# Triangular inversion by 16-blocks, one per partition, laid out by strided 32x32 transposes on VectorE, with one more join, and scans 4 steps apart

## The chip, the cores and the metric

The kernel runs on one core of a Trainium2 chip. The metric is the time of one execution on the device, in microseconds. Before the change it is 3477.72 us, the median of three runs that reach from 3461.62 to 3479.61 us.

## The reference

Everything is fp32, with 256 tokens and a model width of 2048. Two hybrid attention layers come first, then one trunk layer with two recurrent branches (an rwkv7 and a gated delta net), each run in both directions over a context and over the latent tokens, then a merge, a squared-relu MLP and a norm:

```python
for l in range(2):                      # first block
    x = x + concat(fox, diff, moba, gla attention of rms_norm(x) @ w_in[l]) @ w_out[l]
x = rms_norm(x, final_norm_g)
p, pc = modulate(rms_norm(x)) @ in_w, modulate(rms_norm(ctx)) @ in_w   # second block
ya = rwkv7_branch(p, pc); yb = gdn_branch(p, pc)
x = x + g1 * ((gate_a * (ya @ up_a) + gate_b * (yb @ up_b)) @ out_w)
x = x + g2 * (square(relu(modulate(rms_norm(x)) @ mlp_w1)) @ mlp_w2)

# rwkv7_scan, 16 heads of 64, over the tokens, for each direction
sa = S @ kk_t
S = S * dec_t - outer(sa, b_t) + outer(v_t, k_t);   y_t = S @ r_t

# gdn_chunked, 8 heads of 128, chunks of 64 tokens
a_mat = tril(kb @ k.T * decay, -1) + eye(64)
u, w = triangular_solve(a_mat, [v * beta, kb * exp(gc)], lower=True, unit_diagonal=True)
```

The kernel computes both recurrences in chunks of 128 tokens. Written so, each chunk needs the inverse of a unit triangular 128x128 matrix (the identity plus a strictly triangular part), for every head, chunk and direction.

## The kernel before

**Projections.** Most of the work is projections of the tokens by streamed weights. A 128x512 piece of weights is loaded into `wr`, ScalarE casts it to the upper part `wh` (L230) and VectorE subtracts to get the lower part `wl` (L231). For each 128x128 part PE then runs three matmuls into `pp`: upper weights by upper activations (L171), upper by lower (L172), lower by upper (L173). The few `wh` and `wl` buffers are used in turn, so PE stops a little after ScalarE or VectorE stops casting. The row of PE then names `act`, the activations, and `wh` or `wl`.

**Scans.** `scans` (L1637) runs the recurrences as Python generators, four `rwkv` calls (four heads each) and two `gdn` calls (four heads each) for the context ("c"), then the same for the latent tokens ("x"): 12 calls in all. Two calls are alive at a time, in slot 0 and slot 1, and step by turns. The second starts `LEAD` turns after the first (L1641, L1644). The scans are issued at a higher priority than the projections (L1891), which fill what the scans leave.

**What sets the order.** A planner takes the instructions by their priority and by a model of their durations, and writes out one queue per engine (PE, VectorE = DVE, ScalarE = ACT, GpSimd = POOL, SyncE = SP). On the chip every engine then works through its own queue in that fixed order: an instruction that must wait holds up all that stands behind it on its engine. Buffers come from rings: a tile of a tag with `bufs` buffers can be written only when the tile that held the same buffer has been used for the last time. `NN` = 3 is the ring of the tag `nat`, which both slots use, `NL` = 3 that of `LX`.

**One inversion.** Each call inverts 16 matrices of 128x128 at once: 8 (`u`) for each of two directions (`d`), in the tile `nt`, in place. `nt` is filled from score products, which are L1274 in `rwkv` and L1543 in `gdn`. Then `invert` (L1066) does the following.

- VectorE negates the four diagonal 32x32 blocks of each matrix (L1076, L1077), and a 32x32 transpose (L1078) turns those of one direction, so that all have one orientation in `pk`.
- A DMA writes `pk` to DRAM (L1083, `iva`), and two read it back as `X` (L1088), in such a way that one partition holds one 32x32 block: 64 blocks, and each stands on two partitions, one for the even columns and one for the odd. ScalarE copies each partition's 16 columns into `own` (L1093).
- GpSimd does a forward substitution in 30 steps of a multiply (L1099) and an add (L1100). The generator yields every five steps.
- A DMA writes the result to DRAM (L1105, `ivb`), and two read it back as `ivo` in the layout of `nt` (L1113). ScalarE merges even and odd columns into `xb` (L1114), and VectorE transposes it (L1115): now the inverted diagonal blocks are in SBUF both ways.
- First join, 32 to 64: PE multiplies blocks of `nt` by inverted ones (L1126), ScalarE copies from PSUM (L1128), PE multiplies again (L1133, L1134), and ScalarE and VectorE put the parts in place (L1139 to L1145).
- Second join, 64 to 128: the same with 64x64 blocks (L1152, L1154, L1158, L1161).

The small products of the joins use `tile_position`, so that four 32x32 products lie in one matmul array at different places. They are fp32 products, not of the rounded type of the projections.

**The end of the scans.** The last `gdn` call reads its output out through transposes on PE (L1632) and writes `yb` to DRAM. `merge` (L1689) loads it again as `ytb` (L1694), splits it into `yb` pieces, and starts the projection by `up_b`.

Of the kernel before, what the change touches and what calls it, by code (L numbers as in the profile page):

```python
# [9 lines left out]
F32 = mybir.dt.float32  # L10
# [3 lines left out]
AF = mybir.ActivationFunctionType  # L14
ALU = mybir.AluOpType
AX = mybir.AxisListType
# [12 lines left out]

N1, N2, NM = 6, 5, 4  # L30

LEAD = 8

PP, S0, S1 = 3, 3, 2

SCANS = 4000

NN, NL = 3, 3

R0, R1, R2 = 3, 2, 3  # L40

XO = (800, 300, 240, 200)
# [800 lines left out]
class Second:  # L843
# [192 lines left out]
    def scan_consts(self):  # L1036
# [11 lines left out]
        for d in range(2):  # L1048
            sg = 1 if d == 0 else -1
            for base, lst, n in ((-1, self.mst, "mst"), (0, self.min, "min")):  # L1050
                sel(f, on, [[sg, 128]], base, -sg)
                u = c(f"{n}{d}", [128, 128], U8)
                v.tensor_copy(u, f)
                lst.append(u)
        self.srd = [e.t([128, 2, 2, 128], f"srd{j}", 1) for j in range(2)]
        for x in self.srd:
            g.memset(x, 0.0)
# [6 lines left out]
    def invert(self, nt, par):  # L1064
# [9 lines left out]
        iv = lambda n, shape: e.t(shape, n, NN, tag="nat")  # L1074
        for b in range(4):
            v.tensor_scalar(tmp[q(b)], nt[q(b), 0, :, q(b)], -1.0, None, op0=MUL)  # L1076
            v.tensor_scalar(pk[q(b), 1], nt[q(b), 1, :, q(b)], -1.0, None, op0=MUL)  # L1077
        v.transpose(pk[:, 0].rearrange("p u c -> p (u c)"), tmp.rearrange("p u c -> p (u c)"))  # L1078
        da = e.dp.tile([64, 1024], F32, name="iva", tag="iva", bufs=2)
        db = e.dp.tile([128, 512], F32, name="ivb", tag="ivb", bufs=2)  # L1080
        ap = lambda d, *l: bass.AP(tensor=d[:, :].tensor, offset=d[:, :].offset, ap=[list(x) for x in l])

        nc.sync.dma_start(ap(da, (32, 128), (4096, 16), (1, 32)), pk.rearrange("p d u c -> p (d u) c"))  # L1083


        X = e.t([128, 1024], "X", NL, tag="LX")
        for b in range(2):
            nc.sync.dma_start(X[hf(b)], da)  # L1088
        Xm = X.rearrange("p (i j) -> p i j", j=32)
        O = e.t([128, 512], f"own{par}", 1)  # L1090
        Om = O.rearrange("p (i m) -> p i m", m=16)
        for b in range(2):
            s.copy(Om[hf(b)], X.rearrange("p (i m b) -> p i m b", m=16, b=2)[hf(b), :, :, b])  # L1093
        g.memset(O[hf(1), 16:512:33], 0.0)
        yield
        for j in range(1, 31):
            n, w = 31 - j, (j + 1) // 2
            t = e.t([128, 256], f"sub{par}", 1)[:, :n * w].rearrange("p (i c) -> p i c", c=w)
            g.tensor_tensor(t, bc(Xm[:, j + 1:, j], w, 2), bc(Om[:, j, :w], n, 1), op=MUL)  # L1099
            g.tensor_tensor(Om[:, j + 1:, :w], Om[:, j + 1:, :w], t, op=ADD)  # L1100
            if j % 5 == 4:
                yield
        for b in range(2):
            g.memset(O[hf(b), 16 * b:512:33], 1.0)
        nc.sync.dma_start(db, O)  # L1105
        big = e.t([128, 1024], "xb", NL, tag="LX")
        xd, xt = (big[:, i:i + 512].rearrange("p (d u c) -> p d u c", d=2, u=8) for i in (0, 512))

        d64 = e.t([128, 8, 64], "d64", NN, tag="nat")
        g.memset(d64, 0.0)  # L1110
        own = iv("ivo", [128, 16, 2, 16])
        for b in range(2):
            nc.sync.dma_start(own[:, :, b], bass.AP(tensor=db[:, :].tensor, offset=db[:, :].offset + 32768 * b, ap=[[16, 128], [2048, 16], [1, 16]]))  # L1113
        s.copy(big[:, :512].rearrange("p (e m b) -> p e b m", e=16, b=2), own)  # L1114
        v.transpose(xt.rearrange("p d u c -> p (d u c)"), xd.rearrange("p d u c -> p (d u c)"))  # L1115
        db_ = [xd[:, 0], xt[:, 1]]
        xb = [xt[:, 0], xd[:, 1]]
        yield
# [802 lines left out]
```

## Time and profile before

| | |
|---|---|
| median of three runs | 3477.72 us (3461.62 to 3479.61) |
| the profiled execution | 3466.57 us, span 3464.9 us |
| PE (TensorE matmuls) busy | 3271.6 us, 94% of the span |
| PEld (weight loads, beside PE) busy | 2998.4 us, 87% |
| VectorE busy | 2357.9 us, 68% |
| ScalarE busy | 1576.6 us, 46% |
| GpSimd busy | 548.3 us, 16% |
| mean granted TensorE clock | 0.968 of full speed |

The span is the time from the first to the last instruction of one profiled execution. An engine's busy time is the time in which it executes something, its waits and its queue's own work excluded. These shares are means over all stages; the scans lie between about 1200 and 2600 us of the span, and only there does GpSimd have much to do. PE waits are idle times of PE, put down to what ended them. [...]

### The profile page before, as it was taken

What the parts mean: (1) busy time and instruction counts of PE and PEld (TensorE: products, weight loads), DVE (VectorE), ACT (ScalarE), POOL (GpSimd) and SP (SyncE); (2) the same over time, 40 slices, a digit from 0 to 9 for tenths busy, and PEclk for the clock granted to TensorE, in tenths of its full rate; (3) what the DMA queues carried; (4) which work ended last, traced back from release to release, by engine and by line L of the source; (5) the groups of instructions that cost most, each with busy time, mean ns of one, the idle gap of its engine ahead of it and who ended that gap; (6) DMA issues with size and microseconds to landing.
All of it is one profiled execution on the core that took longest, in us unless ns stands there. A gap on an engine that the chain in (4) does not pass through costs nothing. (4 is left out here: it accounts for less than half of the span.)

```text
span 3464.9 us, 71238 instructions
## 1 busy us (share of the span) xinstructions
PE 3271.6 (94%) x27390; PEld 2998.4 (87%) x27390; DVE 2357.9 (68%) x5101; ACT 1576.6 (46%) x3143; POOL 548.3 (16%) x1019
## 2 busy tenths in 40 slices
PE   8999999999999979889798998998889999999998
PEld 6888889878889879888798898898888989899987
DVE  7757766576577778777688686566677655556665
ACT  4444455443444545444344344334344545445553
POOL 1101000001011043333303332322210000001000
PEclk9999999999999989989899999999999999999999
DMA  7677776876765564445545355355555775555554
GB/s 248 220 257 247 253 227 211 277 271 208 246 206 167 174 180 117 138 123 162 149 150 156 103 153 149 121 155 162 169 189 193 243 265 196 189 186 184 186 189 153
DMA packets 302754, 656.10 MB, mean 189 GB/s; under 512 B 99210, under 2 KB 154828, under 8 KB 302284
## 3 DMA queue, kind: packets, MB, share of 16 engines
q1 hardware_dynamic: 302412, 651.54, 59.3%
q8 instruction: 215, 3.52, 0.4%
q14 instruction: 127, 1.04, 0.1%
HBM read 617.22 MB, written 34.22 MB: 188 GB/s over the span
## 5 line engine op out<-in xcount | busy, mean ns | idle before, releaser
L231 DVE TENSOR_TENSOR wl<-wr,wh 128x512 fp32r<-128x512 f32 x1752 | 1228.3, 708 | 721.5 <-ACT wh L230 687.5
L230 ACT CAST wh<-wr 128x512 fp32r<-128x512 f32 x1752 | 1074.9, 619 | 1330.9 <-PE pp L172 846.8
L171 PE MATMUL pp<-act,wh 128*128 128x256 f32 x3920 | 1140.3, 292 | 23.2 <-ACT wh L230 9.9
L173 PE MATMUL pp<-act,wl 128*128 128x256 f32 x3920 | 1137.0, 291 | 5.6 <-DVE wl L231 5.2
L172 PE MATMUL pp<-act,wh 128*128 128x256 f32 x3920 | 1134.0, 290 | 1.6 <-DVE act L929 1.6
L171 PEld LDWEIGHTS pp<-act,wh 128*128 128x128 f32 x3920 | 765.6, 196 | 50.6 <-ACT wh L230 16.3
L173 PEld LDWEIGHTS pp<-act,wl 128*128 128x128 f32 x3920 | 765.2, 195 | 25.9 <-DVE wl L231 9.9
L172 PEld LDWEIGHTS pp<-act,wh 128*128 128x128 f32 x3920 | 766.7, 196 | 13.5 <-issue 7.9
L173 PE MATMUL pp<-mhi,wl 128*128 128x258 f32 x1024 | 291.5, 285 | 0.0
L171 PE MATMUL pp<-mhi,wh 128*128 128x258 f32 x1024 | 290.4, 284 | 0.0
L172 PE MATMUL pp<-mlo,wh 128*128 128x258 f32 x1024 | 288.5, 282 | 0.0
L166 PE MATMUL pp<-act,wh 128*128 128x512 f32 x752 | 266.1, 396 | 0.0
L167 PE MATMUL pp<-act,wl 128*128 128x256 f32 x768 | 212.5, 280 | 1.9 <-DVE wl L231 1.9
L171 PEld LDWEIGHTS pp<-mhi,wh 128*128 128x128 f32 x1024 | 194.6, 190 | 4.5 <-ACT wh L230 3.7
L173 PEld LDWEIGHTS pp<-mhi,wl 128*128 128x128 f32 x1024 | 193.2, 189 | 4.1 <-issue 4.1
L172 PEld LDWEIGHTS pp<-mlo,wh 128*128 128x128 f32 x1024 | 194.5, 190 | 0.5 <-issue 0.4
L1100 POOL TENSOR_TENSOR own<-own,sub 128x30 f32<-128x30 f32 (+4 forms) x360 | 173.7, 482 | 26.7
L1099 POOL TENSOR_TENSOR sub<-X,own 128x30 f32<-128x30 f32 (+4 forms) x360 | 172.1, 478 | 27.8
L166 PEld LDWEIGHTS pp<-act,wh 128*128 128x128 f32 x752 | 141.2, 188 | 31.6
L166 PE MATMUL pp<-u,wh 128*128 128x512 f32 x480 | 168.2, 392 | 0.0
L167 PEld LDWEIGHTS pp<-act,wl 128*128 128x128 f32 x768 | 144.7, 188 | 6.3 <-DVE wl L231 3.5
L1750 POOL TENSOR_TENSOR mrel<-mrelu 128x256 f32<-128x256 f32 x64 | 40.3, 631 | 624.1 <-ACT mrelu L1748 624.1
(514 smaller groups left out, 4704.7 us busy)
## 6 DMA issues: line engine op xcount, KB each, us to landing
wr<-in_in_w SPq DMA_DIRECT2D x252, 512.0 KB, 4.1
wr<-in_w SPq DMA_DIRECT2D x240, 512.0 KB, 4.4
mw<-in_mod_w SPq DMA_DIRECT2D x192, 512.0 KB, 6.0
wr<-in_w1m SPq DMA_DIRECT2D x128, 512.0 KB, 3.8
wr<-in_w2m SPq DMA_DIRECT2D x128, 512.0 KB, 3.7
wr<-in_wo SPq DMA_DIRECT2D x64, 512.0 KB, 4.6
wr<-in_out_w SPq DMA_DIRECT2D x32, 512.0 KB, 3.9
wr<-in_up_a SPq DMA_DIRECT2D x16, 512.0 KB, 4.1
```

The source lines that it names most:

```text
L166: mm(o, hi, h[2][:, k, :], start=k == 0, stop=False)
L167: mm(o[:, :T], lo, h[0][:, k, :], start=False, stop=False)
L171: mm(o, hi, h[0][:, k, :], start=k == 0, stop=False)
L172: mm(o, hi, h[1][:, k, :], start=False, stop=False)
L173: mm(o, lo, h[0][:, k, :], start=False, stop=k == nk - 1)
L230: self.nc.scalar.copy(hi, sl)
L231: self.nc.vector.tensor_tensor(lo, sl, hi, op=SUB)
L1099: g.tensor_tensor(t, bc(Xm[:, j + 1:, j], w, 2), bc(Om[:, j, :w], n, 1), op=MUL)
L1100: g.tensor_tensor(Om[:, j + 1:, :w], Om[:, j + 1:, :w], t, op=ADD)
L1750: g.tensor_tensor(t2, t, t, op=MUL)
```

## The change

The unit of the substitution on GpSimd becomes a 16x16 block, and there are 128 of them (16 matrices by 8 diagonal blocks), one for each partition. They get there and back without DRAM. VectorE's transpose turns each 32x32 square of a 128x512 tile by itself; with an operand whose elements are 32 apart (`p c h u` and `p c h i`, steps through `u` and `c`) it brings the index of the matrix onto the partitions. Each partition then holds both 16x16 diagonal blocks of a 32x32 block, and its own is picked by a multiply with a 0/1 mask, one half on ScalarE, the other added on VectorE. GpSimd copies the block and takes 14 steps; between them it cuts the off-diagonal 16x16 blocks out of `pk` by one masked multiply (`off`). A masked ScalarE copy, a masked VectorE multiply and a strided transpose bring the result back into the layout of `nt`, and a second transpose makes the other orientation.

A new join, 16 to 32, follows: 64 products of 32x32 of `off` by the inverted blocks (L1125 of the changed kernel), a ScalarE copy into `ivh` (L1127), 64 products again (L1130), an add from PSUM and a transpose on VectorE (L1131, L1132). The two joins of before follow as they were. Four of the eight negations at the start go from VectorE to ScalarE (L1082). The two slots start 4 turns apart instead of 8, and the ring `LX`, which now holds one tile per call and no longer two, has 2 buffers.

```diff
-LEAD = 8
+LEAD = 4
-NN, NL = 3, 3
+NN, NL = 3, 2
...
+        self.half, self.other = c("half", [128, 2]), c("other", [128, 2])
+        v.tensor_reduce(self.half, e.fold.rearrange("p (h m) -> p h m", h=2), axis=AX.X, op=ADD)
+        v.memset(self.other[:, 1:], 0.0)
+        v.tensor_copy(self.other[:, :1], self.half[:, 1:])
...
-            v.tensor_scalar(pk[q(b), 1], nt[q(b), 1, :, q(b)], -1.0, None, op0=MUL)
+            s.activation(pk[q(b), 1], nt[q(b), 1, :, q(b)], AF.Copy, scale=-1.0)
         v.transpose(pk[:, 0].rearrange("p u c -> p (u c)"), tmp.rearrange("p u c -> p (u c)"))
...
-        nc.sync.dma_start(ap(da, (32, 128), (4096, 16), (1, 32)), pk.rearrange("p d u c -> p (d u) c"))
-        X = e.t([128, 1024], "X", NL, tag="LX")
-        for b in range(2):
-            nc.sync.dma_start(X[hf(b)], da)
...
-        for b in range(2):
-            s.copy(Om[hf(b)], X.rearrange("p (i m b) -> p i m b", m=16, b=2)[hf(b), :, :, b])
-        g.memset(O[hf(1), 16:512:33], 0.0)
+        pk4 = pk.rearrange("p d u (h c) -> p (d u) h c", h=2)
+        off = e.t([128, 16, 32], f"own{par}", 1)
+        by_half = lambda m: bc(bc(m, 16, 1), 16, 3)
+        tt = iv("ivd", [128, 16, 2, 16])
+        v.transpose(tt.rearrange("p c h i -> p (c h i)"), pk4.rearrange("p u h c -> p c h u"))
+        XO = e.t([128, 2, 16, 16], f"sub{par}", 1)
+        X, O = XO[:, 0], XO[:, 1]
+        s.activation(X, tt[:, :, 0], AF.Copy, scale=self.half[:, 0:1])
+        v.scalar_tensor_tensor(X, tt[:, :, 1], self.half[:, 1:2], X, op0=MUL, op1=ADD)
+        g.tensor_copy(O, X)
         yield
-        for j in range(1, 31):
-            n, w = 31 - j, (j + 1) // 2
...
+        for j in range(1, 15):
+            n = 15 - j
+            t = e.t([128, 64], f"ivn{par}", 1)[:, :n * j].rearrange("p (c i) -> p c i", c=j)
+            g.tensor_tensor(t, bc(X[:, j, j + 1:], j, 1), bc(O[:, :j, j], n, 2), op=MUL)
+            g.tensor_tensor(O[:, :j, j + 1:], O[:, :j, j + 1:], t, op=ADD)
+            if j == 2:
+                g.tensor_tensor(off.rearrange("p u (h c) -> p u h c", h=2), pk4, by_half(self.other), op=MUL)
             if j % 5 == 4:
                 yield
-        for b in range(2):
-            g.memset(O[hf(b), 16 * b:512:33], 1.0)
-        nc.sync.dma_start(db, O)
+        g.memset(XO.rearrange("p a c i -> p (a c i)")[:, 256:512:17], 1.0)
+        z = iv("ivz", [128, 16, 2, 16])
+        s.activation(z[:, :, 0], O, AF.Copy, scale=self.half[:, 0:1])
+        v.tensor_scalar(z[:, :, 1], O, self.half[:, 1:2], None, op0=MUL)
         big = e.t([128, 1024], "xb", NL, tag="LX")
...
+        v.transpose(fd.rearrange("p (u h c) -> p c h u", u=16, h=2), z.rearrange("p c h i -> p (c h i)"))
+        v.transpose(ft, fd)
...
-        own = iv("ivo", [128, 16, 2, 16])
-        for b in range(2):
-            nc.sync.dma_start(own[:, :, b], bass.AP(tensor=db[:, :].tensor, offset=db[:, :].offset + 32768 * b, ap=[[16, 128], [2048, 16], [1, 16]]))
-        s.copy(big[:, :512].rearrange("p (e m b) -> p e b m", e=16, b=2), own)
-        v.transpose(xt.rearrange("p d u c -> p (d u c)"), xd.rearrange("p d u c -> p (d u c)"))
+        yield
+        pT, pD = e.pt(), e.pt()
+        for u in range(16):
+            for b in range(4):
+                mm(s16(pT, u)[q(b)], off[q(b), u, :], s16(ft, u)[q(b)], start=True, stop=True, tile_position=(32 * b, 32 * b))
+        ts = iv("ivh", [128, 512])
+        s.copy(ts, pT)
+        for u in range(16):
+            for b in range(4):
+                mm(s16(pD, u)[q(b)], s16(ts, u)[q(b)], s16(fd, u)[q(b)], start=True, stop=True, tile_position=(32 * b, 32 * b))
+        v.tensor_tensor(fd, fd, pD, op=ADD)
+        v.transpose(ft, fd)
```

Behind `invert` the line numbers of the changed kernel are 17 higher: the score products L1274 and L1543 become L1291 and L1560, the first old join L1126 becomes L1143, its second set L1133 becomes L1150, the read-out transposes L1632 become L1649. In the changed kernel L1090 and L1114 are the strided transposes into and out of the layout by partitions, and L1093 is the ScalarE half of the first masked pick.

The planner's order changes throughout the scans. Three places are shown here, in the rows of the queues (line, operation, out<-in by the program's names, shape, xcount).

PE's queue at the second inversion, which is slot 1's, before: `sm` are the scan's PSUM tiles, L1216 and L1217 are small products of the next call in slot 0, and L1126 is the first join.

```order
L171 MATMUL pp<-act_14795,wh 128x256
L1216 MATMUL sm<-twec,wup 128x256
L1217 MATMUL sm<-xac,aup 128x256
L1216 MATMUL sm<-twec,wup 128x256
L1126 MATMUL sm<-xb,x 32x32 x2
L1217 MATMUL sm<-xac,aup 128x256
L1216 MATMUL sm<-twec,wup 128x256
L1126 MATMUL sm<-xb,x 32x32 x30
L1217 MATMUL sm<-xac,aup 128x256
```

The same place in PE's queue after the change: L1333, L1342 and L1355 belong to the other slot's chunk products, and L1125 is the first set of the new join.

```order
L1333 MATMUL sm<-vs,mk 128x64 x7
L1342 MATMUL sm<-rhs,x 128x64 x8
L1355 MATMUL sm<-ident,kTt 128x128 x2
L1355 MATMUL sm<-ident,bTt 128x128 x2
L1125 MATMUL sm<-xb,own_23665 32x32 x64
L298 MATMUL pp<-ident,rcol 128x128 x2
L171 MATMUL pp<-act_14798,wh 128x256
L172 MATMUL pp<-act_14798,wh 128x256
```

The inversion of slot 1 now falls beside the later part of slot 0's call, not beside the start of its next one. Behind L1125 and the two L298 stand 16 projection rows, and then the second set (L1130, 64 products) comes.

ScalarE's queue at the ninth inversion, before: `th` and the `d_28786` copy are the gates' projection and the first join's own copies, and L1233 and L1234 belong to the other slot.

```order
L230 CAST wh<-wr 128x512 x2
L1019 ACTIVATE th<-pp 128x256
L1114 COPY xb<-ivo 128x16x2x16
L230 CAST wh<-wr 128x512
L1233 ACTIVATE E<-cs,mid 128x129 x2
L1139 COPY d_28786<-xb 32x8x32 x2
L1234 ACTIVATE Ei<-cs,mid 128x129 x2
```

ScalarE's queue at the pair that has the ninth inversion, after: L1082 and L1093 are slot 1's, L1127 is the copy between the new sets of slot 0.

```order
L1082 ACTIVATE pk<-x 32x256 x4
L230 CAST wh<-wr 128x512 x3
L1031 ACTIVATE zsh<-pp 128x256
L1093 ACTIVATE sub_29462<-ivd,half 128x256
L1127 COPY ivh<-sm 128x512
L230 CAST wh<-wr 128x512 x3
L1156 COPY d_29446<-xb 32x8x32 x2
```

L1114 has gone from this queue. In each pair of calls L1127 of slot 0 now stands right behind L1093 of slot 1: `ivh` takes a buffer of the ring `nat`, which slot 1's `pk` and `ivd` hold until then. At the ninth inversion some 370 rows of PE's queue lay between the last score product (L1274) and the first L1126; now there are some 310 between the last L1291 and the first L1125.

PE's queue at the end of the scans, before: L1632 transposes the last read-out, and the projection that follows is that by `up_b`, from the `yb` pieces.

```order
L171 MATMUL pp<-act_31244,wh 128x256
L172 MATMUL pp<-act_31244,wh 128x256
L1632 MATMUL sm<-ident,gosb 128x128 x2
L173 MATMUL pp<-act_31244,wl 128x256
L171 MATMUL pp<-yb_31887,wh 128x256 x3
```

The same place after the change, where L1649 is the read-out's line.

```order
L171 MATMUL pp<-act_32233,wh 128x256
L172 MATMUL pp<-act_32233,wh 128x256
L173 MATMUL pp<-act_32233,wl 128x256
L1649 MATMUL sm<-ident,gosb 128x128 x8
L171 MATMUL pp<-yb_32876,wh 128x256 x3
L172 MATMUL pp<-yb_32876,wh 128x256
```

The scans end later against the projections: after the last score product 181 projection rows stood before (141, then 25 and 15 between the transposes), and now there are 109, all ahead of the transposes.

## Rows read from the trace of the kernel before

**Rows 1.** The page, part 1: busy time, share of the span, instructions.

```profile
PE 3271.6 (94%) x27390; PEld 2998.4 (87%) x27390; DVE 2357.9 (68%) x5101; ACT 1576.6 (46%) x3143; POOL 548.3 (16%) x1019
```

**Rows 2.** The scans: length, busy PE, PEld, DVE, ACT, POOL, clock, DMA share, GB/s.

```profile
1200.00:2600.00 1400.00, 1265.63 (x12277) 1200.66 (x12276) 1025.77 (x2559) 596.18 (x1261) 407.86 (x847) 0.93 0.51 148
```

**Rows 3.** PE's waits from 1150 to 2600: us in total, times, longest.

```profile
PE sm L1126 <- ACT xb L1114: 60.7, 10, 9.3
PE sm L1216 <- DMA wup<-in_wup: 13.8, 2, 8.3
PE pp L171 <- ACT yb L305: 12.5, 1, 12.5
...
PE sm L1133 <- ACT ivs L1128: 2.9, 2, 2.8
```

**Rows 4.** Chain of waits, ninth inversion: start us, us, what.

```profile
2045.41 4.81 DMA iva<-pk
...
2055.68 0.26 POOL sub L1099
...
2092.05 0.23 POOL own L1100
2092.30 2.11 DMA ivb<-own
...
2094.84 4.24 DMA ivo<-ivb
```

**Rows 5.** ScalarE's waits over the span: us in total, times, longest.

```profile
ACT xb L1114 <- DMA ivo<-ivb: 79.9, 12, 12.0
```

**Rows 6.** Timeline of the ninth inversion's end: start us, us, what [idle before].

```profile
2099.10 0.65 ACT L1114 COPY xb<-ivo 128x512 f32<-128x512 f32 x1 [11.25 <-DMA ivo<-ivb]
...
2099.81 0.31 PE L1126 MATMUL sm<-xb,x 32*32 32x32 f32 x4 [8.82 <-ACT xb L1114]
```

**Rows 7.** Six us behind nine PE waits at L1126, first and last.

```profile
1275.40:1281.40 6.00, 6.00 (x143) 5.51 (x145) 5.83 (x17) 4.61 (x11) 0.00 (x0) 0.57 0.67 213
...
2458.00:2464.00 6.00, 5.97 (x113) 5.51 (x113) 5.81 (x16) 4.56 (x11) 0.00 (x0) 0.72 0.71 221
```

**Rows 8.** PE's timeline at the second inversion's first join.

```profile
1344.39 0.72 PE L1126 MATMUL sm<-xb,x 32*32 32x32 f32 x60
1345.04 0.70 PE L1217 MATMUL sm<-xac,aup 128*128 128x256 f32 x2
```

**Rows 9.** PE's timeline behind the eighth inversion's first join.

```profile
1943.05 0.77 PE L1370 MATMUL sm<-ar,srd 128*128 128x128 f32 x2 [1.00 <-DVE vs L1329]
...
1945.54 0.41 PE L172 MATMUL pp<-act,wh 128*128 128x256 f32 x1
1945.75 0.41 PE L173 MATMUL pp<-act,wl 128*128 128x256 f32 x1
...
1955.70 0.28 PE L173 MATMUL pp<-act,wl 128*128 128x256 f32 x1
1955.82 0.28 PE L171 MATMUL pp<-act,wh 128*128 128x256 f32 x1
```

**Rows 10.** Groups by shape, 1200 to 2460: busy us, mean ns | idle before.

```profile
L1099 POOL TENSOR_TENSOR sub<-X,own 128x30 f32<-128x30 f32 x24 | 7.7, 320 | 1.9
...
L1099 POOL TENSOR_TENSOR sub<-X,own 128x56 f32<-128x56 f32 x24 | 8.9, 372 | 1.8
...
L1115 DVE STREAM_TRANSPOSE xb<-xb 128x512 f32<-128x512 f32 x12 | 8.5, 712 | 71.0 <-ACT xb L1114 71.0
...
L1584 DVE TENSOR_TENSOR gyy<-sm,gm 128x512 f32<-128x512 f32 x12 | 8.2, 685 | 2.1 <-PE sm L1582 2.0
...
L1241 DVE SCALAR_TENSOR_TENSOR ar<-k,pv,E 128x256 f32<-128x256 f32 x28 | 13.8, 492 | 0.0
...
L1077 DVE TENSOR_SCALAR pk<-x 32x256 f32<-32x256 f32 x48 | 13.6, 284 | 0.7
...
L1154 ACT COPY iv<-sm 128x512 f32<-128x512 f32 x11 | 6.4, 585 | 10.8 <-PE sm L1152 10.8
```

More of the change, by code (lines that the diff above doesn't have):

```diff
@@ L1076, in invert @@
             v.tensor_scalar(tmp[q(b)], nt[q(b), 0, :, q(b)], -1.0, None, op0=MUL)
-            v.tensor_scalar(pk[q(b), 1], nt[q(b), 1, :, q(b)], -1.0, None, op0=MUL)
+            s.activation(pk[q(b), 1], nt[q(b), 1, :, q(b)], AF.Copy, scale=-1.0)
         v.transpose(pk[:, 0].rearrange("p u c -> p (u c)"), tmp.rearrange("p u c -> p (u c)"))
-        da = e.dp.tile([64, 1024], F32, name="iva", tag="iva", bufs=2)
-        db = e.dp.tile([128, 512], F32, name="ivb", tag="ivb", bufs=2)
-        ap = lambda d, *l: bass.AP(tensor=d[:, :].tensor, offset=d[:, :].offset, ap=[list(x) for x in l])
@@ L1083, in invert @@
-        nc.sync.dma_start(ap(da, (32, 128), (4096, 16), (1, 32)), pk.rearrange("p d u c -> p (d u) c"))
-        X = e.t([128, 1024], "X", NL, tag="LX")
-        for b in range(2):
-            nc.sync.dma_start(X[hf(b)], da)
-        Xm = X.rearrange("p (i j) -> p i j", j=32)
-        O = e.t([128, 512], f"own{par}", 1)
-        Om = O.rearrange("p (i m) -> p i m", m=16)
-        for b in range(2):
-            s.copy(Om[hf(b)], X.rearrange("p (i m b) -> p i m b", m=16, b=2)[hf(b), :, :, b])
-        g.memset(O[hf(1), 16:512:33], 0.0)
@@ L1095, in invert @@
-        yield
-        for j in range(1, 31):
-            n, w = 31 - j, (j + 1) // 2
-            t = e.t([128, 256], f"sub{par}", 1)[:, :n * w].rearrange("p (i c) -> p i c", c=w)
-            g.tensor_tensor(t, bc(Xm[:, j + 1:, j], w, 2), bc(Om[:, j, :w], n, 1), op=MUL)
-            g.tensor_tensor(Om[:, j + 1:, :w], Om[:, j + 1:, :w], t, op=ADD)
+        pk4 = pk.rearrange("p d u (h c) -> p (d u) h c", h=2)
+        off = e.t([128, 16, 32], f"own{par}", 1)
+        by_half = lambda m: bc(bc(m, 16, 1), 16, 3)
@@ L1101, in invert @@
             if j % 5 == 4:
                 yield
-        for b in range(2):
-            g.memset(O[hf(b), 16 * b:512:33], 1.0)
-        nc.sync.dma_start(db, O)
+        g.memset(XO.rearrange("p a c i -> p (a c i)")[:, 256:512:17], 1.0)
+        z = iv("ivz", [128, 16, 2, 16])
+        s.activation(z[:, :, 0], O, AF.Copy, scale=self.half[:, 0:1])
+        v.tensor_scalar(z[:, :, 1], O, self.half[:, 1:2], None, op0=MUL)
         big = e.t([128, 1024], "xb", NL, tag="LX")
         xd, xt = (big[:, i:i + 512].rearrange("p (d u c) -> p d u c", d=2, u=8) for i in (0, 512))
+        fd, ft = (big[:, i:i + 512] for i in (0, 512))
@@ L1115, in invert @@
-        v.transpose(xt.rearrange("p d u c -> p (d u c)"), xd.rearrange("p d u c -> p (d u c)"))
+        yield
+        s16 = lambda x, u: x[:, 32 * u:32 * u + 32]
+        pT, pD = e.pt(), e.pt()
[7 more added lines that the diff above has]
+                mm(s16(pD, u)[q(b)], s16(ts, u)[q(b)], s16(fd, u)[q(b)], start=True, stop=True, tile_position=(32 * b, 32 * b))
```

## The prediction

> **What bounds the kernel now.** I read the shares of the engines first, then the stage that the change touches, then who waits there. TensorE is busy for 94% of the span [rows 1]: whatever else changes, the time follows what TensorE executes, how long it stands, and the clock it is granted. The twelve inversions lie in a stretch of 1400 us in which PE is busy for 1265.6 us, so it stands for 134 us, and its mean granted clock is 0.93 [rows 2]. VectorE is busy for 1025.8 us of that stretch, GpSimd for 407.9: neither is full. The list of PE's waits there has one large entry: 60.7 us, ten times, for L1114, the ScalarE copy that puts the inverted blocks in place for the first join (L1126). No other reaches 14 us [rows 3].
>
> Where this wait comes from is read from one inversion, the ninth, in the chain of waits [rows 4]. The packed blocks are ready at 2045.41; two DMAs bring them to GpSimd, whose first multiply starts at 2055.68, 10.3 us later. GpSimd's sixty steps end at 2092.28 (36.6 us). Two more DMAs and the ScalarE copy follow, and PE starts the join at 2099.81, 7.5 us later. The whole chain takes 54.4 us. ScalarE had been standing at the head of its queue, at L1114, for 11.25 us, that is since 2087.85, and PE for 8.82 us [rows 6]. Over all twelve inversions ScalarE stands there for 79.9 us [rows 5]. The next thing in its queue is a weight cast (the ACT rows in the section on the change), so while it stands no new weights come to PE: that is why a wait of a copy becomes a wait of PE. From the end of GpSimd's last step to L1114 it is 6.8 us in the ninth; twelve times that is 82 us, about the 79.9 that ScalarE stands. On average, then, ScalarE arrives when GpSimd is through, and the wait is the trip through DRAM. In the ninth it arrived 4.4 us earlier, so there half of PE's 8.8 us was GpSimd being late.
>
> After the waits PE is at its lower clock for some microseconds. In the six microseconds behind each of nine such waits the mean granted clock lies between 0.53 and 0.72 ([rows 7] shows the first and the last of the nine); the lost shares of the nine add up to 3.33, times 6 us: 20 us.
>
> **The change, part by part.** The base is the profiled execution, 3466.6 us (span 3464.9), not the median of 3477.72: the three runs reach from 3461.6 to 3479.6, so the base is 0.3% below the median.
>
> (1) The trip through DRAM goes: the four DMA steps, L1093 and L1114. The 60.7 us of PE's wait go with it, and the 20 us of clock behind it: -81 us, if nothing takes their place.
>
> (2) PE gets work. The new join is two sets (L1125, L1130) of 64 products of 32x32 in fp32; the trace shows each fp32 product as two matmuls, so a set is 128. Sixty such matmuls at L1126 hold PE for 0.65 us, from 1344.39 until the next line starts at 1345.04, at full clock [rows 8]. A set is then 128/60 x 0.65 = 1.39 us, and 24 sets are +33 us. None of it is hidden, since PE is the bound. At half clock it would be 67: the bounds are 33 and 67, and I take 33 because PE is at full clock for most of the stretch [rows 2].
>
> (3) The chain becomes short. Ahead of GpSimd stand one 128x512 transpose (0.71 us, as L1115), a ScalarE and a VectorE operation on 128x256 (0.49 each, as L1241): 1.7 us for 10.3. GpSimd does 28 steps on 14 to 56 elements: between 0.32 (30 elements) and 0.37 us (56), with 0.08 between them, 28 x 0.43 = 12 us; the mask on 512 elements and the copy of 256 have no row, and by the slope of these two rows (0.05 us on 26 elements) they are 1.3 and 0.8. Together 14 us for 36.6. Behind come one multiply and two transposes, 0.49 + 2 x 0.71 = 1.9 us for 7.5 [rows 4, 10]. The sum is 17.6 us for 54.4, without queueing. Against this stands the new order: in the ninth inversion about 310 PE rows lie between the last product of its matrix and L1125 (before: about 370 up to L1126). Most are projection matmuls, which start 0.12 us apart at full clock [rows 9]: 37 us of cover for a chain of 18. So the wait should vanish at most inversions. For what remains I scale the 4.4 us by which GpSimd was late in the ninth with the length of its part: 4.4 x 14/36.6 = 1.7 us, at five of twelve inversions: +8 us. Bounds: nothing, and half of what goes, 30 us (the half of the ninth that was GpSimd's).
>
> (4) New handoffs: PE to ScalarE (L1127, 0.59 us, as L1154), back to PE, to VectorE (add from PSUM 0.69, as L1584, and a transpose 0.71), and back. The order puts some twenty projections or the like, 2.4 us, or more into each gap, for 0.6 and 1.4 us of work [rows 9, 10]. The like handoff of today, L1133 after its copy, costs 2.9 us over twelve inversions [rows 3]; two such make +6 us (bounds 0 and 15). ScalarE's L1127 stands directly behind the other slot's L1093; queued behind it are weight casts, on which PE depends. L1093 waits for a VectorE transpose where its predecessor waited for a DMA, so I count nothing more.
>
> (5) Other engines. VectorE gets per inversion three transposes, an add and two multiplies more and gives four small negations to ScalarE: 3 x 0.71 + 0.69 + 2 x 0.49 - 4 x 0.28 = 2.7 us [rows 10], 32 us in all, on 1025.8 of 1400 [rows 2]. The idle 374 us hide it; without that cover it costs 32. SP loses six DMAs per inversion and the waits in front of them; PE does not wait for weights behind them in [rows 3], so nothing is gained there. The smaller `NL` fits: a call now takes one tile of that tag, not two.
>
> [...] L1090 reads and L1114 writes with steps of 32 values; the 0.71 us above are of a transpose without such steps, and no row here shows a strided one. If the two took twice as long, and PE waited for all of it, that would be 12 x 2 x 0.71 = 17 us more, and the sum 3464 instead of 3447.
>
> (6) Clock behind the new sets. A join can lower the clock with hardly a wait: behind a join, at 1943.05, PE had stood for only 1.00 us, and projections still start 0.21 us apart at 1945.75 instead of 0.12 [rows 9]: 2.7 us at half clock, 1.3 lost. If one set in five does this: +6 us (bounds 0 and 32, all 24).
>
> (7) The end of the scans. After the last score product 181 projection rows were left to cover the last read-out (141, then 25 and 15 between its transposes); now there are 109, and none between the transposes (PE rows in the section on the change). That is 72 x 0.12 = 8.6 us less cover in front of PE's 12.5 us wait for `yb` [rows 3]: +8 us (bounds 0 and 9).
>
> Sum: 3466.6 - 81 + 33 + 8 + 6 + 6 + 8 = 3447 us.
>
> **Rivals.** (A) The forecast, 3447. (B) Nothing takes the place: terms 3, 4, 6 and 7 are nil, 3466.6 - 81 + 33 = 3419. For it: 37 us of cover for 18 of chain. Against it: the order of PE is fixed, and every stage of this trace has some wait left. (C) GpSimd, not DRAM, is what is late: half the wait stays, now at L1125 behind a VectorE transpose, 30 us and 10 of clock. 3466.6 - 81 + 40 + 33 + 6 + 6 + 8 = 3479, no change. For it speaks the ninth, where ScalarE came 4.4 us before GpSimd's end; against it the mean over twelve, and that GpSimd's part shrinks most. (D) Slower: the added sets keep PE at its low clock. All 24 run at half clock (+33) and each is followed by 2.7 us at half (+32 in place of 6): 3447 + 59 = 3506. This decides from about 20 of the 24 sets, where the time passes 3495. For it: [rows 9] shows a drop with hardly a wait. Against it: around most new sets projections run without a gap.
>
> **How the numbers follow.** Chances: A 0.47, B 0.20, C 0.23, D 0.10. About 0.5% is what a measurement of this kernel can tell from no change, here 17 us: faster is below 3460, slower above 3495. A and B are faster (0.67), C the same (0.23), D slower (0.10). The range reaches from B, less the 7 us by which runs of one kernel stray from the base, to half way between C and D: 3412 to 3490. A's own range, by the bounds of terms 3, 4, 6 and 7 taken half, is 3430 to 3462.
>
> **What would show it.** Right: in the list of PE's waits L1125 has under 15 us, L1130 and L1143 together under 15, and L1114's ScalarE wait has no successor above 20 us; L1125 and L1130 hold PE for about 33 us; PE stands for about 80 us in the stretch and its mean clock is 0.95 or more. C shows as 30 us or more at L1125, with GpSimd ending last; D as a clock at or below 0.93 with short waits; term 7 as a wait for `yb` of some 20 us. I am wrong if PE's standing time in the stretch does not fall by at least 40 us, or if it falls and the time does not.

## The result and the profile after

The changed kernel takes 3420.23 us (median of four runs, 3413.88 to 3421.40); beside it before took 3472.03 (four runs by then). The ratio is 0.985, 95% interval 0.982 to 0.988: 52 us faster, where 3447 us, some 20 to 25 us faster, was forecast. Two later groups of runs on other chips gave 0.985 and 0.984. Two executions of those later groups, one of before (3935.23 us) and one of e15 (4467.85 us), ran at a mean granted clock of 0.74 and 0.65, and no ratio counts them. The profiled execution took 3419.12 us (span 3417.4).

PE's busy time rose by 15.5 us and the span fell by 47.5 [rows 1]. First part 1 of the page, then the stretch of the scans in the columns of [rows 2]:

```profile
PE 3287.1 (96%) x30462; PEld 3015.2 (88%) x30462; DVE 2360.5 (69%) x5128; ACT 1591.9 (47%) x3191; POOL 352.9 (10%) x635
```

```profile
1200.00:2600.00 1400.00, 1333.83 (x15658) 1264.48 (x15659) 1068.57 (x2667) 639.23 (x1364) 216.10 (x466) 0.95 0.46 144
```

In these 1400 us PE stands for 66 us; it was 134. GpSimd is busy for 216 us instead of 408. The mean granted clock of the whole span went from 0.968 to 0.975: the span times the missing share is 111 us before and 85 after, 25 us less. PE's waits from 1150 to 2600, answering to [rows 3]:

```profile
PE sm L1233 <- DMA wup<-in_wup: 25.4, 4, 9.4
PE pp L171 <- DMA ytb<-ybd: 13.3, 1, 13.3
...
PE sm L1143 <- DVE xb L1131: 1.5, 1, 1.5
...
PE sm L1150 <- issue: 0.9, 1, 0.9
...
PE sm L1130 <- issue: 0.3, 1, 0.3
```

The largest wait of before is gone and at the join nothing stands in its place: L1125 has no entry at all, and L1143 (the old first join), L1150 and L1130 have 3 us together. What leads now are two trips by DMA that were there before, a small weight (L1233 was L1216; 25.4 us for 13.8) and the last read-out's way through DRAM. ScalarE's waits at the inversion, answering to [rows 5], and under them a row of before that the forecast did not read:

```profile
ACT ivz L1109 <- POOL sub L1101: 11.4, 6, 3.2
...
ACT sub L1093 <- DVE ivd L1090: 3.3, 6, 0.8
```

```profile
ACT own L1093 <- DMA X<-iva: 32.5, 19, 5.0
```

Before, ScalarE stood 79.9 us for the trip out (L1114) and 32.5 us for the trip in (L1093), 112 us in all; after, it stands 11.4 us for GpSimd and 3.3 for VectorE, 15 us. The ninth inversion, answering to [rows 4, 6] (timeline: start, duration, what), on VectorE, GpSimd and PE:

```profile
2064.79 0.44 DVE L1083 STREAM_TRANSPOSE pk<-ivt 128x256 f32<-128x256 f32 x1
...
2068.74 1.12 DVE L1090 STREAM_TRANSPOSE ivd<-pk 128x512 f32<-128x512 f32 x1
...
2090.74 1.14 DVE L1114 STREAM_TRANSPOSE xb<-ivz 128x512 f32<-128x512 f32 x1
...
2094.03 0.70 DVE L1115 STREAM_TRANSPOSE xb<-xb 128x512 f32<-128x512 f32 x1
```

```profile
2073.82 0.80 POOL L1095 COPY sub<-sub 128x256 f32<-128x256 f32 x1 [7.08 <-DVE sub L1094]
...
2088.54 0.23 POOL L1101 TENSOR_TENSOR sub<-sub,ivn 128x14 f32<-128x14 f32 x1
```

```profile
2095.16 1.15 PE L1125 MATMUL sm<-xb,own 32*32 32x32 f32 x112
```

From the blocks being ready (2065.23) to PE's first product (2095.16) it is 29.9 us, for 54.4 before and 17.6 forecast. GpSimd takes 15.0 of it, one more than forecast; most of the rest of the excess is queueing (VectorE takes up L1090 3.5 us after L1083). Still PE does not wait, since L1125 stands later in its queue. By the starts and ends of the trace, PE comes to L1125 between 0.4 and 2.6 us behind the end of the last transpose (L1115) at all twelve inversions. Groups by shape, answering to [rows 10]:

```profile
L1125 PE MATMUL sm<-xb,own 32*32 32x32 f32 x1536 | 18.1, 198 | 0.0
L1090 DVE STREAM_TRANSPOSE ivd<-pk 128x512 f32<-128x512 f32 x12 | 13.5, 1127 | 0.0
L1130 PE MATMUL sm<-xb,ivh 32*32 32x32 f32 x1536 | 15.7, 193 | 0.3 <-issue 0.3
L1114 DVE STREAM_TRANSPOSE xb<-ivz 128x512 f32<-128x512 f32 x12 | 13.4, 1116 | 5.7 <-ACT ivz L1109 5.6
L1100 POOL TENSOR_TENSOR ivn<-sub 128x56 f32<-128x56 f32 x24 | 9.4, 393 | 1.9
```

The 24 sets hold PE for 18.1 + 15.7 = 33.8 us, as forecast (33). The two strided transposes take 1.13 and 1.12 us, not 0.71.

### The profile page after: what moved, and what is told of

Same layout as the page of the kernel before. It is cut to its first block, busy times and chain, and to the rows that moved or that the text cites. A ratio compares the mean times of both kernels' runs of the same rounds, so it can differ in the third digit from the quotient of the medians.

```text
span 3417.4 us, 76977 instructions
## 1 busy us (share of the span) xinstructions
PE 3287.1 (96%) x30462; PEld 3015.2 (88%) x30462; DVE 2360.5 (69%) x5128; ACT 1591.9 (47%) x3191; POOL 352.9 (10%) x635
## 4 chain that ended last, share of the span: by engine, by line
PE 83%; DMA 9%; DVE 5%; issue 1%; ACT 1%; POOL 0%; SPq 0%; DVEq 0%; ACTq 0%
PE pp L173 16%; PE pp L171 16%; PE pp L172 16%; PE pp L166 7%; DMA mw<-in_mod_w 4%; PE pp L167 4%; PE mps L891 3%; PE pp L204 2%; PE pp L203 2%; PE pp L205 2%; DVE wl L231 2%; DMA wup<-in_wup 1%; PE sm L1291 1%; PE sm L1321 1%; PE sm L1333 1%
## 5 line engine op out<-in xcount | busy, mean ns | idle before, releaser
L231 DVE TENSOR_TENSOR wl<-wr,wh 128x512 fp32r<-128x512 f32 x1752 | 1220.8, 703 | 690.3 <-ACT wh L230 664.1
L891 PE MATMUL mps<-mw,scw 128*32 128x256 f32 x1536 | 121.7, 390 | 17.9 <-DMA mw<-in_mod_w 17.6
L167 PE MATMUL pp<-u,wl 128*128 128x256 f32 x512 | 138.0, 280 | 0.0
L166 PEld LDWEIGHTS pp<-u,wh 128*128 128x128 f32 x480 | 90.1, 188 | 20.2
```

The source lines that it names most:

```text
L166: mm(o, hi, h[2][:, k, :], start=k == 0, stop=False)
L167: mm(o[:, :T], lo, h[0][:, k, :], start=False, stop=False)
L231: self.nc.vector.tensor_tensor(lo, sl, hi, op=SUB)
L891: nc.tensor.matmul(ps[32 * j:32 * j + 32], self.scw[:, k, :], w[:, j * 256:(j + 1) * 256], start=k == 0, stop=k == NK - 1, tile_position=( ...
```

## The experiments

Times are medians; "ratio" is to before in the same group of runs. The changed kernel itself was run twice more beside others (e9, 3414.82, ratio 0.985; e16, 3409.95, ratio 0.984), and the one with a lead of 8 a second time (e18, 3412.56, ratio 0.984, 0.983 to 0.986). e16 came just below what was expected of it and e18 just above.

> The changed kernel itself, on the chip and beside the same runs of before as the three others, so that they can be compared with it: 3410 to 3425.

> The changed kernel itself, in five rounds on the same chip as the three others, to be compared with: 3410 to 3425.

> The changed kernel with a lead of 8 once more, on the same chip, to be compared with: 3395 to 3412.

**The lead, e1 and e2.** `-LEAD = 4` `+LEAD = 8` in the changed kernel; the reverse in the kernel before.

> The changed kernel with the two slots 8 turns apart, as before. Theory P (PE waits for what comes by DMA, and for hardly anything that an engine makes, because every queue is laid out ahead for the times that engines take, and a trip by DMA takes longer than it was given): the wait at the new join stays below 15 us in all, and the time within 12 us of the changed kernel's 3420. Rival L (the lead of 4 is what covers the inversion): waits of 20 us or more at L1125, and a time of 3440 or more.

> The kernel before with the two slots 4 turns apart and nothing else changed. Theory P: PE's wait for L1114 at L1126 stays between 45 and 80 us (60.7 before), and the time within 15 us of before. Rival L: the wait falls below 35 us and the time by 20 us or more.

e1: 3403.34 us, ratio 0.982 (0.980 to 0.984), 5 us below theory P's band; 2.3 us of wait at L1125. e18 repeated it with 0.984, inside the band. Against 0.984 to 0.985 for a lead of 4 that is 0 to 10 us faster, hardly told from nothing. e2: 3482.05 us, ratio 1.0036 (1.0020 to 1.0052), so the lead of 4 alone costs the kernel before 12.5 us. Its wait at L1126 falls to 40.3, less than theory P had it, but others rise (L1133 from 2.9 to 14.0, L1152 to 10.8): a new order moves waits about. Rival L falls in both: the lead is not what covers the inversion.

**The way out, the way in, and GpSimd's length, e3, e10 and e4.** e3 and e10 each put one DRAM trip back; e4 lengthens GpSimd. The lines left out (`...`) make the DRAM tile and give `z` or `tt` the layout that the trip needs:

```diff
 e3
...
-        v.transpose(fd.rearrange("p (u h c) -> p c h u", ...), z...)
+        nc.sync.dma_start(ap(0, (512, 4), (2048, 32), (1, 512)), z...)
+        for h in range(2):
+            nc.sync.dma_start(own[:, :, h], ap(32768 * h, (16, 128), (2048, 16), (1, 16)))
 e10
...
-        v.transpose(tt..., pk4.rearrange("p u h c -> p c h u"))
+        for h in range(2):
+            nc.sync.dma_start(ap(32768 * h, (16, 128), (2048, 16), (1, 16)), pk4[:, :, h, :])
+        nc.sync.dma_start(tt..., ap(0, (512, 4), (2048, 32), (1, 512)))
...
 e4
-            g.tensor_tensor(t, bc(X[:, j, j + 1:], j, 1), bc(O[:, :j, j], n, 2), op=MUL)
+            for _ in range(5):
+                g.tensor_tensor(t, bc(X[:, j, j + 1:], j, 1), bc(O[:, :j, j], n, 2), op=MUL)
```

> The changed kernel, but the inverted 16-blocks go back to the layout of nt through DRAM (one DMA out, two in, as before) in place of the strided transpose L1114; the short substitution, the way in, the new join and the lead stay. Theory P: PE waits again at L1125, some 4 to 6 us at each of twelve inversions, 45 to 75 us in all, its clock falls behind these waits, and the time goes up to 3470 to 3510. Rival G (the wait went because the chain shrank from 54 to 18 us under some 37 us of projections): the chain is then 23 us, still under its cover, so L1125 waits for less than 15 us in all and the time is below 3435.

> The changed kernel, but the negated blocks go to the layout by partitions through DRAM (two DMAs out, one in) in place of the strided transpose L1090; the way back stays without DRAM. Theory R (PE waits for the excess: the time by which a chain takes longer on the chip than its queue's order allows, a few us for a trip by DMA and 0.08 us for the gap behind each GpSimd instruction; before, ScalarE stood 2.7 us for the trip in and 6.7 for GpSimd and the trip out, at each inversion): 2 to 3 us late at each of twelve, 15 to 40 us slower than the changed kernel. Rival Q (only what lies behind GpSimd counts, since a late start is made up in the cover): less than 10 us slower.

> The changed kernel with each multiply of the substitution on GpSimd done five times (same result): 14 x 6 steps of about 0.43 us, 36 us for an inversion, as long as before the change (36.6). Theory P: PE's wait at L1125 stays below 20 us in all and the time within 15 us of the changed kernel's 3420, since the layout of the queues allows for engine time. Rival G: the chain is 42 us against some 37 of cover, so PE waits for 30 us or more at L1125, and the time is 3455 or more.

e3: 3467.92 us, ratio 1.000 (0.998 to 1.002): one trip takes back the whole gain. Theory P had put 45 to 75 us of wait and 3470 us or more, so it came out a little high; rival G's below 15 us and below 3435 did not come. The waits of e3, VectorE's and PE's (the new join's first set is L1131 there):

```profile
DVE xb L1121 <- DMA xb<-ivb: 48.4, 12, 6.3
...
PE sm L1131 <- DVE xb L1121: 34.1, 11, 5.0
```

e10: 3475.12, ratio 1.0027 (1.0009 to 1.0044), 61 us slower than the changed kernel, where theory R had 15 to 40. PE's wait shows up two steps later, at the old join (L1148), not at the new one:

```profile
ACT sub L1098 <- DMA ivd<-iva: 49.2, 12, 5.8
...
PE sm L1148 <- DVE xb L1136: 26.7, 7, 5.2
...
ACT ivz L1114 <- POOL sub L1106: 17.6, 6, 3.9
```

e4: 3476.15, ratio 1.0028 (1.0013 to 1.0043):

```profile
ACT ivz L1110 <- POOL sub L1102: 75.9, 12, 9.4
...
PE sm L1126 <- DVE xb L1116: 28.2, 7, 5.5
```

P, which trusted engines to come when the order has them, missed e4: with 84 short steps GpSimd is 6.3 us late each time. Rival G named the time but as a matter of length under cover, and e3 and e10 go against it: from the packed blocks to the new join's first product it is 39 us in both, on average over the twelve inversions, 33 in the changed kernel and 55 before, and yet e3 and e10 take as long as before. What fits all three is lateness: the time for which the engine at the chain's next step stands. That GpSimd, busy for longer, costs time in e4 by slowing VectorE is not borne out by its trace: L231 takes 0.700 us on average there from 1170 to 2500 us, and 0.699 in the changed kernel. Rival Q falls with e10.

**Does lateness add up? e13 and e17.** Both trips together, at a lead of 4 and of 8.

> The changed kernel with both ways, in and out, through DRAM again. The way out alone cost 53 us, for 48 us in which VectorE stood for it, and the way in alone 60, for 49 us in which ScalarE stood. Theory R (each microsecond by which the chain is late costs about one in the end, wherever in the chain it arises): the two add up, 95 to 125 us slower than the changed kernel, 3510 to 3545. Rival S (once the chain is late a second delay hides behind the first, or the order finds new cover): 45 to 80 us slower, 3460 to 3498.

> The changed kernel with a lead of 8, as the kernel before has it, and both ways through DRAM. Theory R: a microsecond by which the chain is late costs about one, at this lead too: VectorE and ScalarE stand some 105 to 120 us longer for the two trips, and the kernel is 100 to 130 us slower than with lead 8 alone, 3500 to 3535. Rival S (the price of 1 belongs to the lead of 4, in which the pair's inversions hold each other up): 35 to 85 us slower, 3438 to 3490.

e13: 3534.17 us, ratio 1.020 (1.017 to 1.022). e17: 3534.07, ratio 1.019 (1.018 to 1.021), 121 us slower than e18 beside it. Waits of e13, then of e17:

```profile
DVE xb L1126 <- DMA xb<-ivb: 55.9, 12, 7.1
ACT sub L1098 <- DMA ivd<-iva: 55.6, 12, 7.3
...
ACT ivz L1115 <- POOL sub L1106: 20.0, 6, 4.2
```

```profile
ACT sub L1098 <- DMA ivd<-iva: 59.8, 12, 6.6
...
DVE xb L1126 <- DMA xb<-ivb: 56.9, 11, 7.5
...
ACT ivz L1115 <- POOL sub L1106: 32.0, 9, 6.8
```

Lateness is, for each kernel, the sum of what ScalarE or VectorE stands for the way in, for GpSimd, and for the way out; the changed kernel has 3.3 + 11.4 = 14.7 us (e18 14.2). The ways in of e3 and e4 have 5.9 and 4.7, e3's GpSimd 12.0.

| run | more lateness | more time (ratios x 3467) | price |
|---|---|---|---|
| e3, way out | 51.6 | 52 | 1.0 |
| e10, way in | 52.1 | 61 | 1.2 |
| e4, GpSimd | 65.9 | 62 | 0.9 |
| e13, both ways, lead 4 | 116.8 | 123 | 1.05 |
| e17, both ways, lead 8 | 134.5 | 121 | 0.9 |

With some 10 us of uncertainty in each difference, all agree with a price of about one. The first three are what the price was read from; e13 and e17 were forecast by it and came inside its bands. So theory R stands and rival S falls. The price holds between kernels whose order is otherwise alike, and lateness is not the only cost. e2 has 70 us of it, 42 less than before, and is slower all the same, since its new order has other waits:

```profile
ACT xb L1114 <- DMA ivo<-ivb: 37.3, 6, 11.1
...
ACT own L1093 <- DMA X<-iva: 33.1, 20, 7.1
```

e11, the next run, has less lateness than the changed kernel and is 82 us slower. PE's wait at the join alone would have said 34, 27 and 28 us for the first three, about half.

**Length without steps, e11.**

```diff
+            flat = XO.rearrange("p a c i -> p (a c i)")
+            for _ in range(1 + (j % 3 == 0)):
+                g.tensor_tensor(e.t([128, 512], "more", 1), flat, flat, op=MUL)
```

> The changed kernel with GpSimd made as long as in the run with fivefold multiplies (some 36 us at an inversion), but by 18 added instructions on 512 elements (products into a tile that nothing reads), not 56 on up to 56 elements. Theory R: the lateness comes from the gaps of 0.08 us between GpSimd instructions, 18 more of them where that run had 56 more: PE's waits at L1125 below 12 us, and about a third of that run's 56 us, 5 to 30 us slower than the changed kernel. Rival G (the length of GpSimd's part counts): 28 us or more of wait at L1125, and 45 us or more slower.

3497.39 us, ratio 1.009 (1.006 to 1.011), slower than both theories gave. As R had it, PE does not wait for the data of the new join, and ScalarE stands only 6.6 us for GpSimd; the cost came from elsewhere. VectorE's subtraction (L231), in the changed kernel from 1170 to 2500 us, and then in e11, with the added instruction and PE's wait for the subtraction:

```profile
L231 DVE TENSOR_TENSOR wl<-wr,wh 128x512 fp32r<-128x512 f32 x520 | 360.1, 699 | 125.1 <-ACT wh L230 115.8 <-PE pp L173 4.6 <-PE pp L172 1.2
```

```profile
L231 DVE TENSOR_TENSOR wl<-wr,wh 128x512 fp32r<-128x512 f32 x492 | 381.6, 786 | 121.0 <-ACT wh L230 116.1 <-PE pp L173 1.9
...
L1103 POOL TENSOR_TENSOR more<-sub 128x512 f32<-128x512 f32 x216 | 257.2, 1191 | 3.7
...
PE pp L173 <- DVE wl L231: 17.6, 16, 2.2
```

It takes 0.786 us on average for 0.699, and PE stands for it 16 times, 17.6 us in all (0.2 us in the changed kernel). That this makes up the whole 82 us is not shown. So e11 does not measure what it was made for, and what made e4's steps late (the gaps between them, or the steps themselves) stays open.

**The price of the sets, e5 and e14.** e5 issues both loops of 64 products twice; e14 drops the first and has `s.copy(ts, ft)` for `s.copy(ts, pT)`.

> The changed kernel with both sets of the new join issued twice (same result): 24 sets more on PE. If a set costs the 1.39 us of the forecast and nothing hides it: 33 us more, 3445 to 3465. Rival D (the sets keep PE at its lower clock): 3475 or more, with more time at half clock than in the changed kernel. Rival H (the sets fill gaps in which PE stands anyway): below 3435.

> The changed kernel without the first set of the new join (L1125): ScalarE copies the inverted blocks in place of its products, so 12 of the 24 sets are left out and the inverse is not the reference's. If a set costs the 1.4 us for which it holds PE: 17 us less, 3393 to 3405. Rival D (a set also costs clock): 3390 or less. Rival H (the sets fill gaps): 3408 or more.

e5: 3540.00 us, ratio 1.020 (1.017 to 1.023): 120 us more, not 33. PE's timeline at one doubled set, and its largest such waits:

```profile
1271.28 1.25 PE L1133 MATMUL sm<-xb,ivh 32*32 32x32 f32 x126
...
1272.39 1.19 PE L1136 MATMUL sm<-xb,ivh 32*32 32x32 f32 x120
1276.04 0.26 PE L1136 MATMUL sm<-xb,ivh 32*32 32x32 f32 x6 [2.46 <-issue]
...
1276.59 0.42 PE L173 MATMUL pp<-act,wl 128*128 128x256 f32 x1
1276.81 0.41 PE L171 MATMUL pp<-act,wh 128*128 128x256 f32 x1
```

```profile
PE sm L1136 <- issue: 35.4, 12, 4.2
...
PE sm L1128 <- issue: 24.2, 11, 3.0
```

After 250 of these products in a row PE stands for 2.46 us, put down to issue, that is, to nothing that the list of waits shows, and then projections start 0.22 us apart, at a granted clock of 0.53 from 1276.1 to 1279. Over the two doubled sets of twelve inversions it stands so for 60 us. The DMA queues give a reading of what it stands for. The queue that carries instructions, in before, in the changed kernel and in e5 (pieces, MB, share of the DMA engines):

```profile
q8 instruction: 215, 3.52, 0.4%
...
q8 instruction: 239, 3.92, 0.5%
...
q8 instruction: 263, 4.31, 0.5%
```

It brings one piece of 16 KB for each 256 matmuls and weight loads of PE (54780, 60924 and 67068 of them). A set of 128 passes is 256 of these, and a piece takes 0.97 us on its way (the median in e5). All 23 stands end between 1.2 and 1.6 us after the end of such a piece. My reading is that PE stands for its own code; no run tests that by itself. So rival D's time came, but not for the reason that D gave, and doubling back to back measures something else than a set. e14: 3386.38, ratio 0.977 (0.975 to 0.980), 25 us less than e16 beside it, a time in rival D's band. The stretch of the scans, from its first small product to the first `yb` product, in e14 and in e16 (columns of [rows 2]):

```profile
1150.10:2483.50 1333.40, 1258.97 (x13757) 1193.77 (x13757) 1029.55 (x2634) 612.89 (x1327) 197.85 (x452) 0.95 0.45 144
```

```profile
1162.50:2513.10 1350.60, 1286.05 (x15294) 1219.49 (x15294) 1031.18 (x2634) 614.53 (x1327) 196.03 (x452) 0.94 0.45 142
```

It is 17.2 us shorter, and PE's busy time falls by 27. A set costs between 1.4 us (17.2 / 12) and 2.1 us (25 / 12) by these two readings, so 24 cost 33 to 50 us, and the 33 us of the forecast is a lower end.

**Strides, e6 and e15.** `v.transpose(tt..., pk...)` and `v.transpose(fd, z...)` without the strided views.

> The changed kernel with plain transposes in place of the two strided ones, L1090 and L1114, so the blocks come in a wrong order and the inverse is not the reference's. VectorE's operation falls from 1.12 us to about 0.70, 10 us over 24. If VectorE's steps are off the path that sets the end: 3408 to 3430. Rival (PE waits for the strided part, as the forecast weighed it): 3403 or less.

> The changed kernel with plain transposes in place of the strided ones once more (wrong order of blocks), in five rounds beside the changed kernel. If the strided transposes' 10 us of VectorE are off the path: within 6 us of the changed kernel. If they are on it: 10 to 20 us faster.

e6: 3404.62, ratio 0.982 (0.980 to 0.984), which left it open. e15: 3412.05, ratio 0.985 (0.982 to 0.987), against 3409.95 for e16 beside it: no difference. The plain transposes in e6:

```profile
L1114 DVE STREAM_TRANSPOSE xb<-ivz 128x512 f32<-128x512 f32 x12 | 8.4, 703 | 5.7 <-ACT ivz L1109 5.6
L1090 DVE STREAM_TRANSPOSE ivd<-pk 128x512 f32<-128x512 f32 x12 | 8.4, 699 | 0.0
```

So with steps of 32 values these transposes took 1.6 times the duration (1.12 us, and 0.70 without), 24 x 0.42 = 10 us of VectorE, and the kernel's time does not show it. The 17 us that the prediction weighed for transposes of twice the duration did not come: VectorE is busy for 1068.57 of the 1400 us of the stretch, so it had idle time for the 10.

**What is left, e7, e8 and e12.** A fourth buffer (`NN` 4); the small weights `wup` and `aup` loaded one call ahead, with lead 8; all three. e8 and e12 also take buffers from the ring `p2`: it has 5 in the changed kernel, 4 in e8 and 3 in e12. The weights' edit:

```diff
-N1, N2, NM = 6, 5, 4
+N1, N2, NM = 6, 4, 4
...
-        wu = ld("wup", ...); au = ld("aup", ...)
+        wu, au = self.ups.pop(0)
...
+                if t == 1 and d == 1 and not (isx and b == 3):
+                    self.load_ups((b + 1) % 4)
...
```

> The changed kernel with a fourth buffer in the ring that both slots use in the inversion. Theory N (a lead of 4 costs 17 us because the two inversions of a pair fall together and share that ring of three, so that slot 0 waits for slot 1's first part): 3398 to 3411. Rival W (it costs that because calls start closer together, so that the loads of their small weights are waited for, 25.4 us against 13.0 with a lead of 8, and PE is longer at half clock): 3412 to 3428.

> The changed kernel with a lead of 8, and the two small weights of an rwkv call loaded one call ahead into two buffers of their own. If what is left of PE's waits is the trips by DMA that the order gives too little time: the 13.0 us at L1233 fall below 5 us and the time to 3380 to 3397. Rival (another wait takes their place): 3399 to 3412.

> The changed kernel with three edits together: a lead of 8, four buffers in the inversion's ring, and the small weights loaded one call ahead. If the fourth buffer and the lead cure the same cost (the two inversions of a pair in each other's way), the ring adds nothing to the run with lead 8 and weights ahead (3394): 3385 to 3400. If they cure different ones: below 3382.

e7: 3400.93, ratio 0.9805 (0.979 to 0.982), some 15 us better than the changed kernel: theory N's band, and not W, since PE's wait for `wup` does not fall (30.9 us, 25.4 in the changed kernel). The 17 us that N set out from were e1's; with e18 they are 0 to 10. e8: 3393.65, ratio 0.979 (0.977 to 0.981), the fastest here and inside its band: PE no longer waits for `wup` (13.0 us in e1). e12: 3402.13, ratio 0.981 (0.979 to 0.983), above the band of both theories: no gain over e8. Since e12 also has one buffer of `p2` less than e8, that the fourth buffer adds nothing is not shown. e8 beats the changed kernel by some 20 us and before by 74.

## Why the prediction was wrong

The direction and the mechanism of the main term held, the size did not. Over the spans of the two profiled executions, the forecast had PE stand 39 us less (-60.7 + 8 + 6 + 8) and be busy 19 us more (33 - 20 + 6). It stands 63 us less (193 before, 130 after) and is busy 15.5 us more. So 24 of the 28 us by which the forecast fell short are standing time. The signs that it named came: no wait at L1125, 34 us of PE for the sets, 66 us of standing in the stretch where it had about 80, and a clock of 0.95.

**The step that failed** is what the forecast put in place of the old wait: terms 3, 4, 6 and 7, together +28 us. They came to about 1 us that the traces put down to them.

- Term 3 (+8 for a remaining wait) came to nothing. Scaling the wait of the ninth inversion took cover to be a matter of chance; PE came to L1125 right behind its data at all twelve.
- Term 4 (+6) came to nothing: 3.2 us at L1130, L1143 and L1150 for the 2.9 us that L1133 had before.
- Term 7 (+8) was 0.8 us: the wait for the last read-out is 13.3 us for 12.5.
- Term 6 (+6) is not seen. In the six microseconds behind ten of the twelve first sets, and behind all twelve second ones, the granted clock is 1.00. Behind two first sets it is low, 0.70 and 0.82, which is 3 us lost. But ahead of the one it was at 0.50 already, and in the other PE had stood for 1.91 us for VectorE. The two stretches, answering to [rows 7], and what stands ahead of the drops:

```profile
1301.00:1307.00 6.00, 5.76 (x223) 5.49 (x213) 4.67 (x21) 2.46 (x5) 0.00 (x0) 0.70 0.01 3
...
2096.00:2102.00 6.00, 4.09 (x72) 3.56 (x60) 4.36 (x11) 1.23 (x2) 0.00 (x0) 0.82 0.55 181
```

```profile
1296.00:1299.00 3.00, 3.00 (x15) 3.00 (x16) 3.00 (x9) 1.06 (x3) 0.36 (x1) 0.50 0.24 73
```

```profile
2098.23 0.61 PE L1279 MATMUL sm<-pv,kr 128*128 128x2 f32 x4 [1.91 <-DVE kr L1276]
```

The other terms:

- Term 1 (-81) held in PE's account: 60.7 us of wait to none, and 25 us of clock for 20. What it missed is ScalarE's 32.5 us at L1093 for the trip in. The forecast put that trip into the chain's length, where cover hides it, and gave it no price; e10 shows that a trip in alone costs 61 us, and that PE pays for it at another line. By the price of one the two trips were worth 98 us (112.4 to 14.7 us of lateness), not 81. How much of the 52 us this is cannot be told: no wait of PE in the kernel before names that trip.
- Term 2 held (33.8 us of PE for 33), with 50 us for the sets as the upper reading of e14, and term 5 too: VectorE's added work is hidden.
- No term had the rest of PE's waits. From 1150 to 2600 us the one for `wup` grew by 11.6 us, and all others together fell by 19.
- The lead had no term of its own. In the changed kernel a lead of 4 costs between 0 and 10 us (e1, e18). The 12.5 us of e2 cannot be put in its place, since e2's lateness fell by 42 us at the same time.

Rival B, that nothing takes the place, gave 3419, the measured time, and it was right on the step that failed. That the trip in, the lead and the waits that it does not name nearly cancel is luck. Rival C, whose half wait at L1125 was to be GpSimd's, had its sign in the trace (ScalarE waits 11.4 us for GpSimd), but not at PE. Of D little came: the upper reading of e14 leaves at most 0.7 us a set beyond its time on PE.

Two runs with a lead of 8 can be set beside before without the lead in between. e18 has 98 us less lateness than before and 33 us for the sets: -65 us, and -54 was measured (-63 in e1). e17 has 36 us more lateness (148.7 for 112.4) and the sets: 69 us, and 66 were measured. That agrees, within what the sets are uncertain by, and proves no single term. Why a microsecond of lateness costs PE a whole one, when its own wait shows about half, is only partly seen: against the changed kernel PE stands 37 us longer in e3 and 79 us longer in e13, at many lines, and is busy 13 and 40 us longer, with the clock lower (the span's mean is 0.959 in e13, 0.975 in the changed kernel).

## What to carry to other kernels

Where each engine works through a fixed queue, price a late step by the standing time of the engine that takes the data first, added up over the whole chain, and not by the wait that the bounding engine shows at the end: here, between kernels whose order was otherwise alike, each microsecond of that cost about one of the whole (0.9 to 1.2 in five runs), while PE's own wait showed about half (34, 27 and 28 us of 52, 61 and 62). Before pricing what replaces a wait, ask whether the order has room for it; where all twelve places have some, no average remainder is due. And a constant changed beside the main edit, as the lead, deserves a term and a run of its own.

## What the runs showed of the hardware

- In the changed kernel's 24 single sets of 128 passes (a weight load and a matmul each) PE stood for 0.3 us in all put down to issue (2.3 us in e9; 6.8 us at the second sets of e11), but in e5, after some 250 passes in a row, it stood for 2.46 us (up to 4.2). The queue that carries instructions brought 215, 239 and 263 pieces of 16 KB in before, the changed kernel and e5, one for 256 matmuls and weight loads of PE, and each of 23 such stands in e5 ended 1.2 to 1.6 us after the end of a piece.
- VectorE's 128x512 subtraction L231 took 0.685 us on average where GpSimd stood, 0.766 beside the long substitution of before, 0.717 beside the short one, and 0.964 beside e11's 512-element products (from 1200 to 2460 us; subtractions with over 80% of their time beside a GpSimd operation, against those with under 5%). e11 alone is an experiment on this: its mean went from 0.699 to 0.786 us with the added products.
- The transpose of 128x512 in 32x32 squares took 1.12 us with steps of 32 values on one side (L1090 and L1114 in the changed kernel) and 0.70 without (the same lines in e6).
